# A two-block transformer kernel: convolution taps on VectorE unpinned and given low priority, eight tap tiles for GpSimd, 30 diagonal taps on TensorE, and broadcasts without diagonals

## The chip, the core and the metric

The kernel runs on one core of one Trainium2 chip. The core has five engines that work side by side, each through its own queue in order: TensorE (PE in the profile, with PEld for its weight loads), VectorE (DVE), ScalarE (ACT), GpSimd (POOL) and SyncE (SP, which issues most DMAs). Results of TensorE go to PSUM, eight banks of 128 x 512 fp32; all other tiles lie in SBUF. The metric is the device time of one execution in microseconds, the median of several runs.

## What is computed

Two blocks over a sequence of 512 tokens of width 1024, all in fp32. The first block: RMS norm, a mixer of four mLSTM heads and four gated-linear-attention heads (both directions), a projection, then a feed-forward part with a three-tap convolution. The second block has two layers: a pool-and-convolution mixer, cross-attention to a memory of 256 rows and a feed-forward part; then latent attention, cross-attention and a feed-forward part again; last a norm. Two places matter here.

In the mLSTM each head and direction has, per query t and key s, a decay that is an exponential of a stabilised difference:

```python
d_intra = where(causal, b[t] - b[s] + i[s], -inf)
m_t = maximum(m_inter, max(d_intra, -1))
s = einsum('bhtd,bhsd->bhts', q_, k_) * exp(d_intra - m_t)
```

In the pool-and-convolution mixer the convolution has 31 taps per channel over 512 channels, which the kernel holds as four chunks of 128 channels (one per partition):

```python
gl = glu_a * sigmoid(glu_b)
cv = causal_dwconv(gl, dw_w) + dw_b        # 31 taps per channel
yb = silu(layernorm(cv, ln_g, ln_b))
return concatenate([ya, yb], -1) @ w_out   # ya: pooled windows of 2, 4, 8, 16
```

## The kernel before

Activations are kept transposed, features on partitions and 512 tokens along the free axis. Every large product is made from two-part numbers: `split` (L200 to L216) writes a high part with ScalarE (L208, `wh`) and the remainder with VectorE (L209, `wl`), and `mm3` (L237 to L239) runs three float32r products high x high, low x high, high x low. So each weight tile of 128 x 1024 that TensorE uses costs one operation on ScalarE and one on VectorE before it.

The program is traced in Python and a list scheduler of the language lays out each engine's queue ahead of time: an operation carries a priority from its place in the program, `tc.high_priority(offset=n)` moves that priority by n places earlier (a negative n later), and `tc.keep_in_program_order` (called `pin` here) ties an operation behind the one traced just before it on its engine. The queues are then fixed; on the chip an engine whose next operation waits stands still.

`bcast_cols` (L312 to L326) makes a row that is the same on all partitions from a column: four times, VectorE multiplies the identity by the column (L317, `dg`), and TensorE multiplies a matrix of ones by that diagonal (L318); ScalarE copies the result out as `rb` (L325). It is called at 13 places, in the norms at the ends of the stages.

In the mLSTM, `mx` (L750) holds the running maxima that two scans write (L760, L762). Two additions follow (L764, L765), whose result TensorE transposes (L768). For each of eight head-and-direction pairs `ml_build` spreads one row of `mx` over all partitions with an fp32 product, `mb` (L907), which ScalarE then takes through the exponential (L921).

In the pool-and-convolution stage (`pool_mix`, from L1232) the order of the work is written out in `ORDER`: blocks of the input projection (`a`, `b`, `p`), the pooled windows' products (`w`), and pieces of the next cross-attention's memory projection as filling (`k`). Between them, `all_taps` hands out the taps of chunks 0 to 3, eight at a time. A tap goes one of three ways: `own` taps (`POOLC`, 9, 8, 5 and 3 of the chunks) are scaled by ScalarE into a tile `cm` (L1294, four tiles) and added by GpSimd (L1295), both pinned; `dia` taps (`PEC`, 0, 8, 8 and 8) are fp32 products of TensorE with a diagonal matrix (L1272, L1279); all others are VectorE's, which multiplies and adds into the same PSUM bank (L1303), pinned. L1307 joins the sums into `cv`. `means` (L1368) sums each `cv` over channels with TensorE; after the fourth, the layer norm follows: mean (L1411), difference (L1415), squares (L1417), their sums (L1419), `rsqrt_mean`, `bcast_cols`, gain (L1436) and SiLU (L1438), beside the first products of the output projection.

Of the kernel before, what the change touches and what calls it, by code (L numbers as in the profile page):

```python
# [10 lines left out]
F32 = mybir.dt.float32  # L11
F32R = mybir.dt.float32r
U8 = mybir.dt.uint8
I32 = mybir.dt.int32
ACTF = mybir.ActivationFunctionType
ALU = mybir.AluOpType
# [3 lines left out]
P = 128  # L20
S = 512
# [2 lines left out]
DEC = (3, 6)  # L24
LAG = 0
POOLC = (9, 8, 5, 3)
PEC = (0, 8, 8, 8)
ORDER = 'a1 p3 b2 k a2 p2 k b3 a3 p1 k p0 w3 k w2 w1 w0'
KVS = (0, 2, 0, 1)
TURN = (((2,), (0,)), ((1, 3),))  # L30
# [32 lines left out]
def kernel(ctx: ExitStack, tc: tile.TileContext, A, out, stages=ALL_STAGES):  # L63
    nc = tc.nc
    V, SC, GP, PE, DMA = nc.vector, nc.scalar, nc.gpsimd, nc.tensor, nc.sync
# [25 lines left out]
    def ptmp(shape=(P, S), dtype=F32, tag="t", bufs=6):  # L91
        return tp.tile(list(shape), dtype, tag=tag, bufs=bufs, name=tag)
# [11 lines left out]
    ident = const.tile([P, P], F32, name="ident")  # L104
    ones = const.tile([P, P], F32, name="ones")
# [206 lines left out]
    def bcast_cols(r, m=4, pool=None, stay=False):  # L312

        ps = pm("aux", (P, m * P))
        for j in range(m):
            dg = ptmp((P, P), tag="dg", bufs=2)
            V.tensor_scalar(out=dg, in0=ident, scalar1=r[:, j:j + 1], scalar2=None, op0=ALU.mult)  # L317
            PE.matmul(ps[:, j * P:(j + 1) * P], lhsT=ones, rhs=dg, start=True, stop=True)  # L318
        if stay:
            return ps  # L320
        if pool is None:
            rb = ptmp((P, m * P), tag="rb", bufs=2)
        else:
            rb = pool.tile([P, m * P], F32, tag="rbp", name="rbp")
        SC.activation(out=rb, in_=ps, func=ACTF.Copy)  # L325
        return rb  # L326
# [332 lines left out]
    def mix_heads(mp, layers):  # L659
# [19 lines left out]
        with nc.allow_non_contiguous_dma(reason="a column of 128 for each of 8 feature tiles"):  # L679
            (SC, DMA, GP)[LQ].dma_start(out=par[:, base["mix_pre"]:base["mix_pre"] + KD],  # L680
                         in_=A["norm_mix_pre"].rearrange("o (z p) -> p (o z)", p=P))
# [7 lines left out]
                      in_=wi[:, g0:g0 + 16].rearrange("(k p) c -> p k c", p=P))  # L689
        DMA.dma_start(out=wst[:, :, 16:48],  # L690
                      in_=wi[:, l0:l0 + 32].rearrange("(k p) c -> p k c", p=P))
# [36 lines left out]
        ps = opened[1][0]  # L728
# [6 lines left out]
        def log_sigmoid(dst, x, t):  # L735
# [11 lines left out]

        bt = ptmp()
        um = ptmp()
        mx = mp.tile([P, S], F32, name="mx")  # L750
        GP.memset(um, 0.0)
        GP.memset(mx, 0.0)
        bo = one.to_broadcast([P, S])
# [1 line left out]
                             op0=ALU.mult, op1=ALU.add)  # L755
# [5 lines left out]
                             op0=ALU.mult, op1=ALU.max)  # L761
        V.tensor_tensor_scan(out=mx[64:68, ::-1], data0=bo[32:36], data1=um[32:36, ::-1],  # L762
                             initial=0.0, op0=ALU.mult, op1=ALU.max)
        V.tensor_tensor(out=um[64:68], in0=bt[0:4], in1=mx[0:4], op=ALU.add)  # L764
        V.tensor_tensor(out=um[96:100], in0=bt[64:68], in1=mx[64:68], op=ALU.add)  # L765
        ps = pm("aux")
# [4 lines left out]
        for d in range(2):  # L771
            V.tensor_copy(umc[:, :, 4 * d:4 * d + 4], psv[:, :, 32 * d:32 * d + 4])
            SC.activation(out=em[:, :, 4 * d:4 * d + 4], in_=psv[:, :, 64 + 32 * d:68 + 32 * d],
                          func=ACTF.Exp, scale=-1.0)
# [125 lines left out]
        def span(d, j):  # L900
            return (j * P, S) if d == 0 else (0, (j + 1) * P)

        def ml_build(h, d):
            q, k2 = qs[h], khl[h]
            mb = pm("aux")
            r0 = 64 * d + h
            PE.matmul(mb, lhsT=ident[:, r0:r0 + 1].to_broadcast([P, P]), rhs=mx, start=True,  # L907
                      stop=True)
            e = w5("e", (P, 1280))
            for js in GRP[d]:  # L910
                st = pm("st")
                o0 = OFF[d][js[0]]
                tot = 0
                for j in js:
                    a, b = span(d, j)
                    o = OFF[d][j] - o0
                    ks = slice(j * P, (j + 1) * P)
                    for i in range(2):
                        PE.matmul(st[:, o:o + b - a], lhsT=k2[:, i, ks], rhs=q[:, a:b],
                                  start=i == 0, stop=i == 1)  # L920
                    SC.activation(out=e[:, OFF[d][j]:OFF[d][j] + b - a], in_=mb[:, a:b],  # L921
                                  func=ACTF.Exp, scale=-1.0,
                                  bias=umc[:, j, 4 * d + h:4 * d + h + 1])
                    tot += b - a
                sl = slice(o0, o0 + tot)
                V.tensor_tensor(out=e[:, sl], in0=st[:, :tot], in1=e[:, sl], op=ALU.mult)
                for j in js:
                    a, b = span(d, j)
                    o = OFF[d][j] + (0 if d == 0 else b - a - P)
                    sg = 1 if d == 0 else -1  # L930
                    GP.affine_select(out=e[:, o:o + P], in_=e[:, o:o + P], pattern=[[sg, P]],
                                     compare_op=ALU.is_ge, fill=0.0, base=0,
                                     channel_multiplier=-sg)
            return e
# [300 lines left out]
    def pool_mix(nm, nxt, pp, fill):  # L1235
# [32 lines left out]
        def diagonals(c):  # L1268
            dgs[c] = []
            for j in dia[c]:  # L1270
                dg = pp.tile([P, P], F32, tag="dgc", bufs=10, name="dgc")
                SC.activation(out=dg, in_=ident, func=ACTF.Copy, scale=pc("dw_w", 4 * j + c))  # L1272
                dgs[c].append(dg)

# [6 lines left out]

        pin = tc.keep_in_program_order

        def conv(c):
            gl, ps = gls[c], cps[c]
            c2 = pp.tile([P, S], F32, tag="c2", bufs=2, name="c2")
            SC.activation(out=c2, in_=gl[:, 0:S], func=ACTF.Identity, scale=pc("dw_w", c),
                          bias=pc("dw_b", c))
            fresh = not PEC[c]
            for j in range(1, 31):  # L1290
                w = pc("dw_w", 4 * j + c)
                if j in own[c]:
                    t = pp.tile([P, S], F32, tag="cm", bufs=4, name="cm")
                    pin(SC.activation(out=t, in_=gl[:, j:j + S], func=ACTF.Copy, scale=w))  # L1294
                    pin(GP.tensor_tensor(out=c2, in0=c2, in1=t, op=ALU.add))  # L1295
                elif j in dia[c]:
                    continue
                elif fresh:
                    V.tensor_scalar(out=ps, in0=gl[:, j:j + S], scalar1=w, scalar2=None,
                                    op0=ALU.mult)  # L1300
                    fresh = False
                else:
                    pin(V.scalar_tensor_tensor(out=ps, in0=gl[:, j:j + S], scalar=w, in1=ps,  # L1303
                                               op0=ALU.mult, op1=ALU.add))
                yield
            cv = pp.tile([P, S], F32, name=f"cv{c}")
            V.tensor_tensor(out=cv, in0=ps, in1=c2, op=ALU.add)  # L1307
            cvs[c] = cv
            yield
# [104 lines left out]
        for c in range(4):  # L1414
            V.tensor_tensor(out=cvs[c], in0=cvs[c], in1=mean, op=ALU.subtract)  # L1415
            sq = ptmp(tag="sq", bufs=3)
            SC.activation(out=sq, in_=cvs[c], func=ACTF.Square)  # L1417
            for j in range(4):
                PE.matmul(pss[:, j:j + 1], lhsT=sq[:, j * P:(j + 1) * P], rhs=ones[:, 0:1],  # L1419
                          start=c == 0 and j == 0, stop=c == 3 and j == 3)  # L1420
# [10 lines left out]
        r = rsqrt_mean(pss, S, 4)  # L1431
# [3 lines left out]
        for c in range(4):  # L1435
            V.scalar_tensor_tensor(out=cvs[c], in0=cvs[c], scalar=pc("ln_g", c), in1=lb,  # L1436
                                   op0=ALU.mult, op1=ALU.mult)
# [383 lines left out]
    pcs, pp = ExitStack(), []  # L1821
# [78 lines left out]
```

## Time and profile before

| | us |
|---|---|
| median of 3 runs | 2183.96 |
| lowest and highest | 2183.51 and 2189.16 |
| the profiled execution | 2181.3 |
| its span in the trace | 2178.9 |

| engine | busy us | share of the span |
|---|---|---|
| TensorE | 2105.1 | 97% |
| TensorE's weight loads | 1768.7 | 81% |
| VectorE | 1208.9 | 55% |
| ScalarE | 945.9 | 43% |
| GpSimd | 372.7 | 17% |

The profiled execution is 2.7 us below the median, and its span leaves out 2.4 us around the work. Shares are averages over stages that differ; a stage is read in windows of time. The mLSTM lies at about 40 to 200 us, the pool-and-convolution stage at about 786 to 935 us. The granted clock is that of TensorE as a share of its full speed.

### The profile page before, as it was taken

What the parts mean: (1) busy time and instruction counts of PE and PEld (TensorE: products, weight loads), DVE (VectorE), ACT (ScalarE), POOL (GpSimd) and SP (SyncE); (2) the same over time, 40 slices, a digit from 0 to 9 for tenths busy, and PEclk for the clock granted to TensorE, in tenths of its full rate; (3) what the DMA queues carried; (4) which work ended last, traced back from release to release, by engine and by line L of the source; (5) the groups of instructions that cost most, each with busy time, mean ns of one, the idle gap of its engine ahead of it and who ended that gap; (6) DMA issues with size and microseconds to landing.
All of it is one profiled execution on the core that took longest, in us unless ns stands there. A gap on an engine that the chain in (4) does not pass through costs nothing.

```text
span 2178.9 us, 27908 instructions
## 1 busy us (share of the span) xinstructions
PE 2105.1 (97%) x10807; PEld 1768.7 (81%) x10807; DVE 1208.9 (55%) x1795; ACT 945.9 (43%) x1561; POOL 372.7 (17%) x414
## 2 busy tenths in 40 slices
PE   7999899999999999899999999999999999999998
PEld 6888778788888876778888888888888888888887
DVE  6655755655532378755665554337885565555432
ACT  5765554433332454343443333226774343333322
POOL 2113411211100047020111110112322011111010
PEclk9999999999999999999999999999999999999999
DMA  5543245233333332532233333331124223333331
GB/s 144 161 152 114 88 145 165 73 102 97 97 112 98 114 102 82 174 118 77 73 92 97 97 97 96 116 107 45 35 93 151 78 58 87 97 97 97 94 102 66
DMA packets 369984, 222.88 MB, mean 102 GB/s; under 512 B 22407, under 2 KB 351036, under 8 KB 369852
## 3 DMA queue, kind: packets, MB, share of 16 engines
q1 hardware_dynamic: 366304, 219.65, 33.9%
q8 instruction: 85, 1.39, 0.3%
q10 hardware_dynamic: 3228, 1.42, 0.2%
q14 instruction: 47, 0.39, 0.1%
q0 software_dynamic: 320, 0.04, 0.0%
HBM read 201.41 MB, written 19.66 MB: 101 GB/s over the span
## 4 chain that ended last, share of the span: by engine, by line
PE 80%; DVE 8%; ACT 5%; issue 3%; POOL 1%; DMA 1%; SPq 0%; ACTq 0%; POOLq 0%; DVEq 0%
PE mm L239 21%; PE mm L237 21%; PE mm L238 21%; PE st L237 2%; PE st L238 2%; PE st L239 2%; PE nd L237 2%; PE nd L238 2%; PE nd L239 1%; DVE wl L209 1%; ACT wh L208 1%; DVE cv L1303 1%; ACT pr L1727 1%; PE aux L318 1%; DVE c L1726 1%
## 5 line engine op out<-in xcount | busy, mean ns | idle before, releaser
L208 ACT ACTIVATE wh<-ws 128x1024 fp32r<-128x1024 f32 (+2 forms) x352 | 361.3, 1029 | 774.1 <-PE mm L239 556.7
L209 DVE TENSOR_TENSOR wl<-ws,wh 128x1024 fp32r<-128x1024 f32 (+2 forms) x352 | 421.9, 1200 | 335.7 <-ACT wh L208 335.4
L237 PE MATMUL mm<-a,wh 128*128 128x512 f32 (+1 forms) x1364 | 530.2, 389 | 2.8 <-ACT a L208 1.3
L239 PE MATMUL mm<-a,wh 128*128 128x512 f32 (+1 forms) x1364 | 528.1, 387 | 1.6 <-DVE a L215 1.6
L238 PE MATMUL mm<-a,wl 128*128 128x512 f32 (+1 forms) x1364 | 527.9, 387 | 0.8 <-DVE wl L209 0.8
L237 PEld LDWEIGHTS mm<-a,wh 128*128 128x128 f32 x1364 | 258.4, 190 | 54.7 <-ACT a L208 1.7
L239 PEld LDWEIGHTS mm<-a,wh 128*128 128x128 f32 x1364 | 258.2, 189 | 54.0 <-DVE a L215 3.4
L238 PEld LDWEIGHTS mm<-a,wl 128*128 128x128 f32 x1364 | 258.3, 189 | 51.6 <-DVE wl L209 2.0
L237 PE MATMUL mm<-hh,wh 128*128 128x512 f32 (+1 forms) x550 | 209.6, 381 | 0.0
L238 PE MATMUL mm<-hh,wl 128*128 128x512 f32 (+1 forms) x550 | 209.3, 381 | 0.0
L239 PE MATMUL mm<-hl,wh 128*128 128x512 f32 (+1 forms) x550 | 209.3, 381 | 0.0
L283 POOL TENSOR_TENSOR sq<-sq 128x512 f32<-128x512 f32 x60 | 92.4, 1540 | 646.6 <-ACT sq L278 562.0
L1203 POOL TENSOR_TENSOR t<-t,rb 128x512 f32<-128x512 f32 x66 | 85.1, 1290 | 613.9 <-ACT t L1202 613.9
L1190 DVE TENSOR_TENSOR t<-mm,rb 128x512 f32<-128x512 f32 x64 | 44.2, 691 | 147.2 <-PE mm L239 147.2
L1206 DVE TENSOR_TENSOR t<-mm,t 128x512 f32<-128x512 f32 x65 | 45.0, 692 | 140.4 <-POOL t L1203 140.4
L239 PEld LDWEIGHTS mm<-hl,wh 128*128 128x128 f32 x550 | 103.4, 188 | 19.8
L238 PEld LDWEIGHTS mm<-hh,wl 128*128 128x128 f32 x550 | 103.4, 188 | 19.7
L237 PEld LDWEIGHTS mm<-hh,wh 128*128 128x128 f32 x550 | 103.4, 188 | 19.6
L237 PE MATMUL mm<-wh,a 128*128 128x256 f32 x346 | 100.1, 290 | 2.3 <-DVE Kl L209 2.3
L239 PE MATMUL mm<-wl,a 128*128 128x256 f32 x346 | 99.6, 288 | 1.8 <-DVE wl L209 1.7
L1199 DVE SCALAR_TENSOR_TENSOR t<-t,par 128x511 f32<-128x511 f32 (+1 forms) x132 | 98.7, 748 | 3.2 <-ACT t L1195 0.9
L1202 ACT ACTIVATE t<-t 128x512 f32<-128x512 f32 x66 | 41.7, 632 | 133.6 <-DVE t L1199 133.5
(469 smaller groups left out, 3553.3 us busy)
## 6 DMA issues: line engine op xcount, KB each, us to landing
ws<-in_ffn_w_up_dram SPq DMA_DIRECT2D x110, 512.0 KB, 3.8
ws<-in_ffn_w_down_dram SPq DMA_DIRECT2D x48, 512.0 KB, 3.8
ws<-in_xa_wkv_dram SPq DMA_DIRECT2D x32, 512.0 KB, 4.4
ws<-in_w_in_dram SPq DMA_DIRECT2D x24, 512.0 KB, 5.0
ws<-in_ffn_w_gate_dram SPq DMA_DIRECT2D x22, 512.0 KB
ws<-in_ffn_w_down_dram SPq DMA_DIRECT2D x24, 384.0 KB, 3.4
ws<-in_xa_wq_dram SPq DMA_DIRECT2D x16, 512.0 KB, 5.5
ws<-in_xa_wo_dram SPq DMA_DIRECT2D x16, 512.0 KB, 3.7
```

The source lines that it names most:

```text
L208: SC.activation(out=hi, in_=src, func=ACTF.Copy)
L209: eng.tensor_tensor(out=lo, in0=src, in1=hi.bitcast(F32), op=ALU.subtract)
L237: PE.matmul(ps, lhsT=lh, rhs=rh, start=start, stop=False)
L238: PE.matmul(ps, lhsT=ll, rhs=rh, start=False, stop=False)
L239: PE.matmul(ps, lhsT=lh, rhs=rl, start=False, stop=stop)
L283: GP.tensor_tensor(out=self.acc, in0=self.acc, in1=self.new, op=ALU.add)
L318: PE.matmul(ps[:, j * P:(j + 1) * P], lhsT=ones, rhs=dg, start=True, stop=True)
L1190: V.tensor_tensor(out=g, in0=pg, in1=rb, op=ALU.mult)
L1199: V.scalar_tensor_tensor(out=cv[:, o], in0=g[:, i], scalar=w, in1=cv[:, o], op0=ALU.mult, op1=ALU.add)
L1202: SC.activation(out=ge, in_=cv, func=func)
L1203: GP.tensor_tensor(out=ge, in0=ge, in1=rb, op=ALU.mult)
L1206: V.tensor_tensor(out=h, in0=pu, in1=ge, op=ALU.mult)
```

## The change

Four edits. (1) `bcast_cols` has no diagonal any more: the column itself, read as if it were 128 equal columns, is the stationary operand and the identity the moving one. (2) `mx` moves to a temporary tile and is split into a float32r tile `mhl`, high parts in its own rows (one ScalarE copy) and remainders 32 rows below (two VectorE subtractions); a selector `sel`, the identity plus itself moved by 32, adds both parts in one float32r product per `mb`, where there was an fp32 product. (3) GpSimd's taps get eight tiles in a fixed round, five of `cm` and three borrowed from the ring of `sq`; VectorE's taps are no longer pinned, and their priority is 120 places later than their place in the program. (4) `PEC` goes from 24 to 30 diagonal taps, so VectorE's taps go from 71 to 65 (one of them, L1299, opens chunk 0), and the ring of diagonals from 10 to 11 tiles.

```diff
-PEC = (0, 8, 8, 8)
+PEC = (0, 9, 10, 11)
@@ bcast_cols
         for j in range(m):
-            dg = ptmp((P, P), tag="dg", bufs=2)
-            V.tensor_scalar(out=dg, in0=ident, scalar1=r[:, j:j + 1], scalar2=None, op0=ALU.mult)
-            PE.matmul(ps[:, j * P:(j + 1) * P], lhsT=ones, rhs=dg, start=True, stop=True)
+            PE.matmul(ps[:, j * P:(j + 1) * P], lhsT=r[:, j:j + 1].to_broadcast([P, P]), rhs=ident,
+                      start=True, stop=True)
@@ mix_heads
-        mx = mp.tile([P, S], F32, name="mx")
+        mx = ptmp()
+        mhl = mp.tile([P, S], F32R, name="mx")
+        sel = ptmp((P, P), F32R, tag="dg", bufs=2)
...
+        SC.activation(out=mhl, in_=mx, func=ACTF.Copy)
+        for r0 in (0, 64):
+            V.tensor_tensor(out=mhl[r0 + 32:r0 + 36], in0=mx[r0:r0 + 4],
+                            in1=mhl[r0:r0 + 4].bitcast(F32), op=ALU.subtract)
+        V.tensor_tensor(out=sel[:, 0:96], in0=ident[:, 0:96], in1=ident[:, 32:P], op=ALU.add)
@@ ml_build
-            PE.matmul(mb, lhsT=ident[:, r0:r0 + 1].to_broadcast([P, P]), rhs=mx, start=True,
+            PE.matmul(mb, lhsT=sel[:, r0:r0 + 1].to_broadcast([P, P]), rhs=mhl, start=True,
                       stop=True)
@@ diagonals
-                dg = pp.tile([P, P], F32, tag="dgc", bufs=10, name="dgc")
+                dg = pp.tile([P, P], F32, tag="dgc", bufs=11, name="dgc")
@@ pool_mix
+        def tap_tiles():
+            while True:
+                for n in range(8):
+                    yield ptmp(tag="sq", bufs=3) if n % 3 == 2 or n == 7 else \
+                        pp.tile([P, S], F32, tag="cm", bufs=5, name="cm")
+
+        cms = tap_tiles()
@@ conv
-                    t = pp.tile([P, S], F32, tag="cm", bufs=4, name="cm")
+                    t = next(cms)
                     pin(SC.activation(out=t, in_=gl[:, j:j + S], func=ACTF.Copy, scale=w))
                     pin(GP.tensor_tensor(out=c2, in0=c2, in1=t, op=ALU.add))
...
-                    pin(V.scalar_tensor_tensor(out=ps, in0=gl[:, j:j + S], scalar=w, in1=ps,
-                                               op0=ALU.mult, op1=ALU.add))
+                    with tc.high_priority(offset=-120):
+                        V.scalar_tensor_tensor(out=ps, in0=gl[:, j:j + S], scalar=w, in1=ps,
+                                               op0=ALU.mult, op1=ALU.add)
```

## Rows read from the trace of the kernel before

**Rows 1.** The page, busy time: engine, us, share of the span, instructions.
```profile
PE 2105.1 (97%) x10807; PEld 1768.7 (81%) x10807; DVE 1208.9 (55%) x1795; ACT 945.9 (43%) x1561; POOL 372.7 (17%) x414
```
**Rows 2.** The page, the chain that ended last: shares of the span by engine.
```profile
PE 80%; DVE 8%; ACT 5%; issue 3%; POOL 1%; DMA 1%; SPq 0%; ACTq 0%; POOLq 0%; DVEq 0%
```
**Rows 3.** Waits of PE, whole span: total us, times, longest us.
```profile
PE aux L1368 <- DVE cv L1307: 7.0, 3, 3.2
...
PE aux L768 <- DVE t L765: 3.5, 1, 3.5
PE aux L318 <- DVE dg L317: 3.5, 6, 1.0
...
PE mm L239 <- DVE wl L209: 1.7, 3, 0.7
```
**Rows 4.** Windows: length, then busy us of PE, PEld, DVE, ACT, POOL, clock, DMA.
```profile
50.00:200.00 150.00, 143.55 (x1032) 129.56 (x1031) 92.72 (x199) 105.79 (x216) 27.53 (x51) 0.99 0.45 139
802.60:907.00 104.40, 95.96 (x472) 72.81 (x470) 87.53 (x114) 44.84 (x69) 52.62 (x49) 0.98 0.31 99
835.40:838.80 3.40, 3.36 (x4) 1.51 (x5) 3.33 (x5) 1.03 (x2) 2.09 (x3) 0.50 0.47 154
913.60:920.60 7.00, 7.00 (x28) 6.13 (x27) 1.94 (x5) 1.64 (x3) 0.00 (x0) 0.52 0.97 315
```
**Rows 5.** Timeline of PE, pool-and-convolution stage: start, us, operation, idle before it.
```profile
835.44 2.04 PE L1368 MATMUL aux<-cv,ones 128*128 128x512 f32 x2 [3.03 <-DVE cv L1307]
907.02 2.03 PE L1368 MATMUL aux<-cv,ones 128*128 128x512 f32 x2 [3.25 <-DVE cv L1307]
913.12 1.16 PE L1419 MATMUL aux<-ones,sq 128*128 128x1 f32 x8 [2.79 <-ACT sq L1417]
930.86 0.50 PE L237 MATMUL mm<-a,wh 128*128 128x512 f32 x1 [1.32 <-ACT a L208]
```
**Rows 6.** Chain that ended last, by time: start, us on the chain, what.
```profile
31.49 0.64 ACT t L737
42.59 0.69 DVE t L765
120.86 0.86 PE aux L907 x2
779.84 0.23 PE op L237
802.78 6.87 PE cv L1279 x16
```
**Rows 7.** Lines L907, L317, L318: instructions, ns minimum, median, maximum.
```profile
L907 PEld LDWEIGHTS aux<-mx,ident x16: 187/188/337, 66.6 to 161.3; 128*128 128x128 f32 x16
L317 DVE TENSOR_SCALAR dg<-ident,c x52: 278/286/316, 18.7 to 1808.7; 128x128 f32<-128x128 f32 x52
L318 PEld LDWEIGHTS aux<-dg,ones x104: 186/189/192, 22.6 to 1809.1; 128*128 128x128 f32 x104
L318 PE MATMUL aux<-dg,ones x104: 270/275/377, 22.8 to 1809.2; 128*128 128x128 f32 x104
```
**Rows 8.** Line L1303, VectorE's taps: instructions, ns minimum, median, maximum.
```profile
L1303 DVE SCALAR_TENSOR_TENSOR cv<-gl,par,cv x70: 740/756/757, 800.8 to 904.5; 128x512 f32<-128x512 f32 x70
```
**Rows 9.** Timeline of DVE, pool-and-convolution stage: start, us, operation, idle before.
```profile
815.17 0.69 DVE L1251 TENSOR_TENSOR t<-mm,rb 128x512 f32<-128x512 f32 x1 [4.51 <-PE mm L239]
...
828.57 1.22 DVE L209 TENSOR_TENSOR wl<-ws,wh 128x1024 fp32r<-128x1024 f32 x1
...
875.37 0.69 DVE L209 TENSOR_TENSOR wl<-ws,wh 128x512 fp32r<-128x512 f32 x1 [2.05 <-ACT wh L208]
```
**Rows 10.** Timeline of POOL, same stage: start, us, operation, how many.
```profile
818.78 14.83 POOL L1295 TENSOR_TENSOR c<-c,cm 128x512 f32<-128x512 f32 x9
...
885.02 1.30 POOL L1295 TENSOR_TENSOR c<-c,cm 128x512 f32<-128x512 f32 x1
```
**Rows 11.** Waits of all engines, 780 to 935 us: total us, times, longest.
```profile
ACT cm L1294 <- POOL c L1295: 4.8, 5, 1.6
```

## The prediction, as it stood before the result was known

> **What bounds the kernel now.** I read the page's busy times first, then the chain that ended last, then TensorE's waits, then windows of the two stages that the change touches, and last the timelines of single engines there. TensorE is busy for 97% of the span and VectorE for 55% [rows 1], and 80% of the chain is TensorE's own work [rows 2]. So two things alone move the end: time that TensorE's queue works, and time that it stands still. All its recorded idle time is 2178.9 - 2105.1 = 73.8 us, spread over the whole program; a change that touches two stages can reach only a part of it. Its largest wait is L1368, the channel sums of a finished convolution chunk, for `cv`: 7.0 us in three waits; L768 behind the running maxima has 3.5 us, L318 behind the diagonals 3.5 us [rows 3]. From 802.6 to 907 us, the convolution, TensorE is idle for 104.4 - 95.96 = 8.4 us, so L1368 is nearly all of that; VectorE is busy for 87.5 us of the 104.4 [rows 4], which is the densest it is anywhere for so long. An idle time costs more than itself: after 3.03 us the pair of L1368 at 835.44 took 2.04 us [rows 5] where an fp32 pair of the same shape takes 0.86 [rows 6], and the granted clock of the 3.4 us from 835.4 was 0.50 (1.2 GHz for 2.4), which loses 1.7 us more [rows 4]; the 3.25 us before 907.02 have the same pair at 2.03 us behind them [rows 5].
>
> **Edit 2, the maxima.** An `mb` is two passes of 0.43 us, 0.86 in all; a float32r product of the same 512 columns holds TensorE for 0.23 us [rows 6]. Its weights are a repeated column before and after, and loading such costs 188 ns, like any others (189) [rows 7]. Eight times 0.63 is 5.04 us less work for TensorE. In the window from 50 to 200 us, where they lie, TensorE is busy for 143.55 of 150 us [rows 4], so I count 96% of it: **-4.8 us** (bounds -5.0, and -2.5 if half of it falls into waits). Against that stand one ScalarE copy, two VectorE subtractions and the selector. The nearest rows are a ScalarE operation of 128x512 at 0.64 and a four-row VectorE addition at 0.69 (L765), on the chain at 42.59 us [rows 6]; the selector is like a `dg`, 0.29 [rows 7]. L764 can run while ScalarE copies, but the two subtractions come before L765 in the program, and TensorE already waits 3.5 us for L765 [rows 3]. So 2 x 0.69 lie on the path, and a little of the selector: **+1.5 us** (bounds 0, if L765 goes first, and 0.64 + 1.38 + 0.29 = 2.3). Who waits there is L768 and all that TensorE has queued behind it. The first `mb` comes over 20 us later, at 66.6 us [rows 7], so that its own new wait, for `mhl`, costs nothing. `mx` in a temporary tile takes one of six; at that time others have had their last reader, so I put nothing on it, and at worst one later step waits for one scan.
>
> **Edit 1, the broadcasts.** 52 operations of 286 ns leave VectorE, 14.9 us in all; TensorE's 104 passes stay with the same shape and load [rows 7]. VectorE's time is off the path except where TensorE waits for a diagonal, 3.5 us in six waits [rows 3]. After the change TensorE waits for the column itself, one VectorE operation earlier; what is queued behind it is the same. I take 70% of the waits: **-2.5 us** (bounds 0 and -3.5).
>
> **Edits 3 and 4, the convolution.** Six more diagonals are six more fp32 products: 16 passes took 6.87 us [rows 6], so 0.86 each, **+5.15 us** of work that TensorE cannot avoid. They take six taps of 756 ns [rows 8], 4.5 us, from VectorE. The six more ScalarE diagonals lie in an engine that is busy for 45 of 104 us [rows 4] and cost nothing.
>
> What the freed taps can give back is read from VectorE's idle time. It stands still four times for long between 810 and 876 us, for 4.51, 2.85, 3.70 and 2.05 us, the first and the last in [rows 9], 13.1 us together, each time for a gate, a split or a part of a window that TensorE or ScalarE had not delivered, while taps whose data lay ready were pinned behind it. Unpinned they fill these gaps. With the six taps gone VectorE is 13.1 + 4.5 = 17.6 us ahead at the last `cv`. GpSimd must keep up: its last addition ends at 886.3 us [rows 10], 20 us before the last `cv` is awaited, and the tiles that made ScalarE wait 4.8 us for GpSimd [rows 11] are doubled. So the waits of L1368 should go. I keep 1.5 of the 7.0 us, since TensorE's queue is laid out ahead of time and each earlier chunk may still come a little late: **-5.5 us**; the two stretches at half clock go with them, 2 x 1.7: **-3.4 us**. Of TensorE's waits for `wl`, 1.7 us in all [rows 3], I take **-0.7**. Net: 5.15 - 5.5 - 3.4 - 0.7 = **-4.45 us**. The layer norm behind the last `cv` keeps its cost in this sum: 2.79 us before the squares' sums, 1.32 before the last products [rows 5], and 7 us at clock 0.52 [rows 4], of which half is lost, together 7.6 us. It shrinks only if the last `cv` comes so early that TensorE still has other products to run. The bounds of this part: nothing comes back, +5.15; everything does, with the tail, 5.15 - 7.0 - 3.4 - 1.3 - 7.6 = -14.2.
>
> One row bears on VectorE and GpSimd side by side. A `wl` at 828.57 us took 1.22 us [rows 9] in the middle of nine GpSimd additions without a gap [rows 10], which is no more than others take. The Trainium skill (SBUF — State Buffer, section "SBUF: two separate sides") says that a VectorE operation with two SBUF inputs and a GpSimd operation that reads SBUF take a shared pair of ports in turn, and the later one waits for the whole of the other. By that rule, more additions in a row would speak against this change; this row does not agree.
>
> **The sum.** -4.8 + 1.5 - 2.5 - 4.45 = -10.25 us. Against the profiled execution, 2181.3 us, that is 2171.0. The median of the runs lies 2.7 us higher, and I carry the difference over: 2183.96 - 10.25 = **2173.7 us**. About 0.3%, 6.55 us, is what a measurement of this kernel can tell from no change: faster is under 2177.4, slower over 2190.5. All bounds on one side give 2183.96 - 5.0 - 3.5 - 14.2 = 2161.3, on the other 2183.96 - 2.5 + 2.3 + 5.15 = 2188.9.
>
> **The rivals.** *The waits stay (0.23).* The queues are fixed by a plan; if VectorE runs later than planned by as much as now, L1368 waits as now. For it: all three of its waits are of this kind, and `po` (L1330) and GpSimd's additions stay pinned behind taps. Against it: 17.6 us of lead. Then the diagonals cost 5.15 and perhaps 1 us comes back: -4.8 + 1.5 - 2.5 + 4.15 = -1.65, **2182.3 us**. *The tail goes too (0.14).* If the 17.6 us of lead reach the layer norm, its 7.6 us are hidden as well: **2166.1 us**. *Taps ahead of weights, slower (0.07).* A plan that takes a `wl` to be ready later than it is puts a tap before it, and TensorE waits. 19 weight splits start between 798.9 and 907 us; each one caught costs up to one tap, 0.756 us, once its reserve is used up. With the waits of the first rival, from (6.55 + 1.65) / 0.756 = 11 of them the kernel is slower by over 0.3%; at 14 it is **2192.9 us**. Against it: low priority puts the taps behind, and TensorE's waits for `wl` are 1.7 us today [rows 3]. *Turns at the ports (0.04).* If each of the 19 splits waited for half of a GpSimd addition of 1.30 us [rows 10], VectorE would lose 12.4 of the 17.6 us; with half of L1368's waits and one half-clock stretch back, 5.2 us more than forecast, **2178.9 us**. This is the rule of the Trainium skill's page on SBUF named above. The row of 828.57 us speaks against it, and TensorE's share of the work doesn't change by it.
>
> **How the numbers follow.** The forecast, some 2168 to 2179 us, has 0.52. Faster: 0.50 of it and the hidden tail, 0.64. Within 0.3%: the rest of it, the waits that stay, the ports and a part of the fourth, 0.31. Slower: 0.05. The range, 2164 to 2184 us, takes in the first rival and most of the second, and leaves out the fourth.
>
> **What would show it.** Right: L907 as one pass of about 0.23 us, eight of them; L317 gone and L318's wait with it; L1303 64 times, in the place of the four idle stretches; L1368 without a wait over 1.5 us and no half clock at its side; 12 more passes of L1279. Wrong: L1368 still waiting 5 us or more (the plan's error, not VectorE's load, set it); new waits for `wl` in the convolution; L768 waiting 2 us longer than 3.5, or not at all longer.

## The result, and the profile after

The changed kernel took **2163.36 us** in the median of five runs (2163.23 to 2167.51), the kernel before 2187.45 us in five runs beside it (2183.51 to 2189.16). The ratio is **0.9897** with an interval of 0.9883 to 0.9911: 22.5 us less (the two medians differ by 24.1; differences below go by the ratios unless medians are named), where the prediction had 10.25 us less. A second measurement later, with more runs of the kernel before beside it (17), gave 0.9930 [0.9912, 0.9947], 15.3 us less (run e9 below). Both lie clear of no change.

The profiled execution of after took 2167.51 us (span 2165.7), that of before 2181.3 (span 2178.9). The pair of profiles therefore shows 13.2 us of span. The profile of before is quicker than each of its five timed runs, that of after is the slowest of its five; a part of the difference between the medians stands in neither profile, and runs e1 and e2 below show a stretch that can hold some of it.

Busy times of after (the page; as [rows 1]), and TensorE's waits over the whole span (as [rows 3]: total us, times, longest):

```profile
PE 2099.2 (97%) x10811; PEld 1770.3 (82%) x10811; DVE 1196.4 (55%) x1740; ACT 947.9 (44%) x1568; POOL 375.1 (17%) x414
```
```profile
PE st L1098 <- DVE xb L1087: 5.5, 2, 3.9
...
PE aux L775 <- DVE t L772: 3.3, 1, 3.3
PE aux L316 <- DVE c L309: 2.5, 4, 0.9
PE aux L1385 <- DVE cv L1324: 2.4, 2, 1.7
...
PE mm L239 <- DVE wl L209: 1.0, 1, 1.0
```

TensorE's idle time falls from 73.8 to 2165.7 - 2099.2 = 66.5 us. The channel sums of the convolution chunks (L1368, now L1385) wait 2.4 us in two waits, not 7.0 in three. The wait of 2.8 us ahead of the squares' sums (L1419, now L1436) is in the list no more. The first line is no cost of the change, though it was 3.0 us before: L1098 lies in the gated-linear-attention part, and kernels whose program is that of before up to there waited 3.0 (e4), 5.5 (e12) and 6.4 us (e3) for the same `xb`. It scatters from one execution to the next.

Along the program the lead of after grows so: the last `mb` ends 6.7 us earlier (162.3 to 155.7 us), the pool-and-convolution stage opens 5.2 us earlier (793.0 to 787.8), and it ends, at the copy of the second broadcast behind it, 13.8 us earlier (976.3 to 962.5). So that stage gives 8.5 us. The 5.2 us are less certain than they look: four kernels with the program of before up to this point (before, e3, e4, e12) open the stage at 791.4 to 797.2 us, the eight with edits 1 and 2 at 787.8 to 792.9. The stage itself is used below as the yardstick: from the first `rb` copy of it to the one behind it, 183.3 us before, 174.7 after. Windows (length; busy us of PE, PEld, DVE, ACT, POOL; clock; DMA), first of before, then of after:

```profile
793.00:976.30 183.30, 170.15 (x801) 132.43 (x800) 131.10 (x182) 83.54 (x127) 70.14 (x61) 0.96 0.39 122
```
```profile
50.00:200.00 150.00, 144.20 (x1072) 134.16 (x1072) 91.87 (x197) 106.52 (x218) 27.29 (x51) 0.99 0.48 146
787.80:962.50 174.70, 169.71 (x809) 132.68 (x808) 127.51 (x168) 85.03 (x133) 70.45 (x61) 0.98 0.42 128
797.30:892.00 94.70, 91.31 (x423) 67.04 (x422) 81.67 (x105) 43.41 (x72) 52.51 (x50) 1.00 0.28 88
904.30:911.10 6.80, 6.80 (x22) 5.65 (x21) 0.90 (x5) 0.00 (x0) 1.02 (x1) 0.50 0.59 188
```

In the stage TensorE's idle time falls from 183.3 - 170.15 = 13.2 to 174.7 - 169.71 = 5.0 us, and the time at half clock from 13.7 us (three stretches) to 6.8 (the one at 904.3). That is 8.2 + 3.4 us of gain against 5.15 us for six more diagonals, 6.5 us net; the other 2.0 of the 8.5 us are not assigned to a row. The convolution itself ran at full clock (1.00 from 797.3 to 892; 0.98 in [rows 4]).

The timeline of TensorE in after (start, us, operation, idle before it; as [rows 5]):

```profile
826.02 1.10 PE L1385 MATMUL aux<-cv,ones 128*128 128x512 f32 x2 [1.72 <-DVE cv L1324]
...
842.87 1.12 PE L1385 MATMUL aux<-cv,ones 128*128 128x512 f32 x2 [0.65 <-DVE cv L1324]
...
865.99 1.02 PE L1385 MATMUL aux<-cv,ones 128*128 128x512 f32 x2
...
892.82 1.02 PE L1385 MATMUL aux<-cv,ones 128*128 128x512 f32 x2
900.63 1.84 PE L1436 MATMUL aux<-ones,sq 128*128 128x1 f32 x16
...
917.82 0.50 PE L237 MATMUL mm<-a,wh 128*128 128x512 f32 x1 [1.10 <-ACT a L208]
```

No pair of L1385 takes 2.03 us any more, the time of such a pair at half clock [rows 5]. The third and the fourth `cv` are there when TensorE comes to them. Most of all: L1436 at 900.63 has no idle time before it. It follows directly on filling products for the next memory projection, the last of them at 900.51. In before those products had run out when the last `cv` came, and TensorE stood still for 2.79 us [rows 5].

VectorE's idle time did not go away, it moved. Its two long waits in the convolution of after (the timeline of DVE; as [rows 9]):

```profile
835.74 3.92 DVE L1320 SCALAR_TENSOR_TENSOR cv<-gl,par,cv 128x512 f32<-128x512 f32 x5 [3.77 <-PE cv L1286]
...
866.19 3.92 DVE L1320 SCALAR_TENSOR_TENSOR cv<-gl,par,cv 128x512 f32<-128x512 f32 x5 [6.38 <-PE cv L1286]
```

Four waits of 13.1 us for gates and splits became two of 10.2 us for the diagonals' products (L1279, now L1286): the taps of a chunk add into the bank that those products open. Set against the start of the stage, the last `cv` comes at 892.6 - 787.8 = 104.8 us where it came at 907.0 - 793.0 = 114.0 before: **9.2 us of lead**, not the 17.6 that the prediction counted.

### The profile page after: what moved, and what is told of

Read it like the earlier page. It is cut to its first block, busy times and chain, and to the rows that moved or that the text cites. A ratio compares the mean times of both kernels' runs of the same rounds, so it can differ in the third digit from the quotient of the medians.

```text
span 2165.7 us, 27870 instructions
## 1 busy us (share of the span) xinstructions
PE 2099.2 (97%) x10811; PEld 1770.3 (82%) x10811; DVE 1196.4 (55%) x1740; ACT 947.9 (44%) x1568; POOL 375.1 (17%) x414
## 4 chain that ended last, share of the span: by engine, by line
PE 81%; DVE 8%; ACT 5%; issue 4%; POOL 1%; DMA 0%; SPq 0%; POOLq 0%; ACTq 0%; DVEq 0%
PE mm L239 21%; PE mm L237 21%; PE mm L238 21%; PE st L237 2%; PE st L239 2%; PE st L238 2%; DVE wl L209 2%; PE nd L237 2%; PE nd L238 1%; PE nd L239 1%; DVE cv L1320 1%; PE cv L1286 1%; ACT wh L208 1%; ACT pr L1744 1%; DVE c L1743 1%
```

## The experiments

Two theories were set against each other. By the first, the parts add up and each is as large as its term of the sum. By the second, the convolution part is worth far more than its term, since an earlier last `cv` also takes the waits and the half clock of the layer norm's tail. Four kernels do one part of the change alone on the kernel before; their runs share the runs of the kernel before (2184.56 us).

**The broadcasts alone** (edit 1).

```diff
-            dg = ptmp((P, P), tag="dg", bufs=2)
-            V.tensor_scalar(out=dg, in0=ident, scalar1=r[:, j:j + 1], scalar2=None, op0=ALU.mult)
-            PE.matmul(ps[:, j * P:(j + 1) * P], lhsT=ones, rhs=dg, start=True, stop=True)
+            PE.matmul(ps[:, j * P:(j + 1) * P], lhsT=r[:, j:j + 1].to_broadcast([P, P]), rhs=ident,
+                      start=True, stop=True)
```

> The kernel before with the first edit alone: column broadcasts without diagonals. Theory A, the terms of the prediction: 2.5 us faster than the kernel before (0 to 3.5), since TensorE's waits for the diagonals (3.5 us) go. Theory B, the gain of 24 us in the medians comes from work taken off VectorE at the ends of stages, which the terms missed: 8 us or more faster. In the trace: rb of each norm 0.5 to 1 us earlier than its reciprocal root was before.

Measured: 2181.84 us, ratio 0.9985 [0.9975, 0.9995], so -3.3 us (-1.1 to -5.5); forecast -2.5. The broadcasts wait 2.4 us in four waits, where they waited 3.5 in six: 1.1 of the 3.3 us can be seen there. The copies `rb` start earlier, as expected: at most of the 11 places 1.25 to 1.4 us behind the end of the reciprocal root, where it was 2.0 to 2.1. Against this stands a wait that grew: in every run with edit 1 TensorE waits 3.6 to 4.6 us for `x` (L480, in the first block), in every run without 0.8 to 1.7 us; two waits for an `a` behind it shrink from 2.5 to 0.7 us in all. The profile of e1 shows something else. The waits around the last `cv` are those of before to the hundredth, and behind them the clock stays at half for 20.5 us in one piece (timeline, then window):

```profile
907.54 1.12 PE L1367 MATMUL aux<-cv,ones 128*128 128x512 f32 x2 [3.25 <-DVE cv L1306]
913.22 1.01 PE L1418 MATMUL aux<-ones,sq 128*128 128x1 f32 x4 [2.79 <-ACT sq L1416]
```
```profile
908.80:929.30 20.50, 17.71 (x57) 14.82 (x58) 6.93 (x15) 5.63 (x11) 1.02 (x1) 0.50 0.59 201
```

20.5 us at 0.50 cost 10 us; the two stretches at the same place in the profiled execution of before, 3.4 and 6.8 us, cost 5. The order of TensorE's products in this stage is that of before up to the broadcast behind the layer norm (in e2, which has the same stretch, all through the stage). So the tail, which the prediction took at 7.6 us from one profile, can cost up to 5 us more in another execution, an estimate from these stretches; the whole stage took 186.4 us in e1 and 187.1 in e2, for 183.3.

**The maxima alone** (edit 2, its core).

```diff
+        SC.activation(out=mhl, in_=mx, func=ACTF.Copy)
+        for r0 in (0, 64):
+            V.tensor_tensor(out=mhl[r0 + 32:r0 + 36], in0=mx[r0:r0 + 4],
+                            in1=mhl[r0:r0 + 4].bitcast(F32), op=ALU.subtract)
...
-            PE.matmul(mb, lhsT=ident[:, r0:r0 + 1].to_broadcast([P, P]), rhs=mx, start=True,
+            PE.matmul(mb, lhsT=sel[:, r0:r0 + 1].to_broadcast([P, P]), rhs=mhl, start=True,
```

> The kernel before with the second edit alone: running maxima split in two parts, one float32r product for each spread row. Theory A, the terms: 4.8 us less work for TensorE, 1.5 us more in front of the transposes, 3.3 us faster. Theory B, that shorter products let ScalarE and VectorE start earlier in each head as well: 6 us or more faster by the end of the mLSTM. In the trace: eight products of 0.23 us in place of 0.86, the wait of the transposes 5 us in place of 3.5.

Measured: 2180.88 us, ratio 0.9978 [0.9966, 0.9990], -4.8 us (-2.2 to -7.4); forecast -3.3. Timelines of DVE and PE:

```profile
40.94 0.68 DVE L772 TENSOR_TENSOR t<-t 4x512 f32<-4x512 f32 x1
41.65 0.68 DVE L773 TENSOR_TENSOR t<-t 4x512 f32<-4x512 f32 x1
42.37 1.38 DVE L769 TENSOR_TENSOR mx<-t,mx 4x512 fp32r<-4x512 f32 x2
```
```profile
42.48 0.63 PE L776 MATMUL aux<-ident,t 128*128 128x128 f32 x4 [3.37 <-DVE t L773]
```

The plan put both additions ahead of the two subtractions that are traced before them (L769 after L772 and L773), and the transposes wait 3.37 us, as before (3.54). So the trace shows the +1.5 us of the prediction to be zero; without it, the term is -4.8. The interval alone would not tell -4.8 from -3.3. This execution has 20.5 us at half clock in the tail as well, from 904.5.

**The convolution alone** (edits 3 and 4), and then **without the six diagonals** (edit 3 alone, `PEC` left at 24).

```diff
-PEC = (0, 8, 8, 8)
+PEC = (0, 9, 10, 11)        # e3 only
...
-                    t = pp.tile([P, S], F32, tag="cm", bufs=4, name="cm")
+                    t = next(cms)
...
-                    pin(V.scalar_tensor_tensor(out=ps, in0=gl[:, j:j + S], scalar=w, in1=ps,
-                                               op0=ALU.mult, op1=ALU.add))
+                    with tc.high_priority(offset=-120):
+                        V.scalar_tensor_tensor(out=ps, in0=gl[:, j:j + S], scalar=w, in1=ps,
+                                               op0=ALU.mult, op1=ALU.add)
```

> The kernel before with the third and fourth edit alone: free low-priority taps, eight tap tiles, 30 diagonal taps. Theory A, the terms: 4.5 us faster, the waits of the channel sums mostly gone, the layer norm's tail as it was. Rival, the tail goes too: 12 us or more faster. Rival, the waits stay: 4 us slower.

> As the run with the third and fourth edit, but with 24 diagonal taps as before, so that VectorE keeps 71 taps and TensorE has 5.15 us less work. Theory A: the freed taps alone give back 9.6 us, and the six diagonals cost 5.15 of them, so this run is about 5 us faster than the run with 30 diagonals. Rival, VectorE is what bounds the convolution once its taps are free: this run is no faster than the one with 30 diagonals, or slower, and the channel sums wait again.

Measured: e3 2168.91 us, 0.9935 [0.9917, 0.9953], **-14.2 us** (forecast -4.45, its lowest bound -14.2); e4 2166.28 us, 0.9914 [0.9900, 0.9927], **-18.8 us**. The three parts, -3.3, -4.8 and -14.2, make -22.3 us, the whole as first measured -22.5; as measured again in e9 it is -15.3, so whether the parts add up is not settled. The convolution is where the forecast fell short: its part alone moved by 9.75 us more than its term. The difference of e3 and e4 is the price of six diagonals: 4.6 us by the ratios and 2.6 by the medians, where the prediction had 5.15. The intervals of the two runs overlap, but their stages agree (172.6 and 168.7 us, below).

The sums and the whole region of the convolution and its tail in e4:

```profile
828.61 1.10 PE L1378 MATMUL aux<-cv,ones 128*128 128x512 f32 x2 [1.33 <-DVE cv L1317]
843.78 1.13 PE L1378 MATMUL aux<-cv,ones 128*128 128x512 f32 x2 [0.69 <-DVE cv L1317]
```
```profile
828.00:932.00 104.00, 99.40 (x511) 78.21 (x512) 82.44 (x115) 47.89 (x72) 34.44 (x34) 1.00 0.43 139
```

The clock is 1.00 through all 104 us, tail included, and no wait stands before the squares' sums. The stage takes 168.7 us in e4 and 172.6 in e3 (183.3 before), with 5.5 and 5.0 us of idle TensorE and no half clock. Against the profile of before, e3 thus has 2.79 us of wait and 6.8 us at half clock less in the tail; with half of the latter lost time, that is 6.2 us that the prediction had left in place. The 3.5 us that remain of the 9.75 can come from longer stretches in other executions of before, as in e1 and e2; no run shows that they do.

**Parts taken out of the change.** Four kernels start from the changed kernel: the diagonals back at 24; the taps of VectorE pinned again; GpSimd's taps back in four `cm` tiles; the taps free but at the priority of their place. They were run together, beside 2183.62 us.

```diff
-PEC = (0, 9, 10, 11)
+PEC = (0, 8, 8, 8)                                                  # e5
...
-                    with tc.high_priority(offset=-120):
-                        V.scalar_tensor_tensor(out=ps, ...)
+                    pin(V.scalar_tensor_tensor(out=ps, ...))         # e6
+                    V.scalar_tensor_tensor(out=ps, ...)              # e8
...
-                    t = next(cms)
+                    t = pp.tile([P, S], F32, tag="cm", bufs=4, name="cm")   # e7
```

> The changed kernel with 24 diagonal taps as before (ring of ten). Theory A, the six diagonals are plain work of TensorE even in the changed kernel, since VectorE has time to spare once its taps are free: 4.5 us faster than the changed kernel, about 22 us + 4.5 = 27 us faster than the kernel before. Rival, six more taps make VectorE late at the last join: the wait of the channel sums comes back by 3 us or more and the run is no faster than the changed kernel.

> The changed kernel with VectorE's taps pinned again, but the eight tiles and the 30 diagonals kept. Theory A, the freed place of the taps is what removes the waits of the channel sums and the half-clock stretches: the waits are back (over 5 us), a half-clock stretch lies behind the last channel sum, and the run is 12 us or more slower than the changed kernel. Rival, the tiles do it, by no longer holding ScalarE: within 4 us of the changed kernel.

> The changed kernel with four tap tiles as before, taps free at low priority, 30 diagonals. Theory A: the tiles matter little, within 3 us of the changed kernel; ScalarE waits for GpSimd 4 to 5 us again without anybody waiting for it. Rival, ScalarE's wait delays weights and windows that the freed taps now depend on: 5 us or more slower, with new waits of TensorE for weights.

> The changed kernel with VectorE's taps free but at their own place's priority, not 120 places later. Theory A, that it is the lifted pin and not the lower priority: within 3 us of the changed kernel. Rival, that taps at their own priority run ahead of the weights' remainders: TensorE's waits for these grow to 5 us or more, and the run is 5 us or more slower than the changed kernel.

Since three of the four came out alike, the changed kernel itself was measured once more (e9), beside 2185.01 us, together with two kernels with still fewer diagonals (`PEC = (0, 6, 6, 6)` and `(0, 4, 4, 4)`, the rest of the change kept).

> The changed kernel once more, beside the kernel before and the three runs of this call, so that 30, 18 and 12 diagonals are compared on one chip. All theories: about 2163 to 2166 us, 0.99 of the kernel before; in the trace no half-clock stretch of more than 7 us in the convolution's tail.

> The changed kernel with 18 diagonal taps (6 each of chunks 1 to 3). Theory A, diagonals are plain TensorE work while VectorE has time to spare: 12 x 0.86 = 10 us less work than the changed kernel, of which at least 5 us show. Rival, VectorE's last join then comes after TensorE has run out of filling: the wait of the last channel sum returns (3 us or more), and with it a half-clock stretch, so that the run is no faster than with 24 diagonals, or slower.

> The changed kernel with 12 diagonal taps (4 each). VectorE has 18 taps, 13.6 us, more than in the changed kernel. Theory A holds on only if VectorE's idle time covers them: 15 us less work of TensorE. Rival, past the point where VectorE is full: the channel sums wait 6 us or more, and the run is slower than with 18.

| kernel | median us | ratio [interval] | stage us | TensorE idle | at half clock |
|---|---|---|---|---|---|
| e9, the change again | 2168.70 | 0.9930 [0.9912, 0.9947] | 172.9 | 5.7 | 3.4 |
| e6, taps pinned | 2168.36 | 0.9931 [0.9914, 0.9947] | 176.0 | 7.1 | 6.8 |
| e7, four tiles | 2168.50 | 0.9931 [0.9910, 0.9952] | 174.4 | 7.0 | 3.4 |
| e8, own priority | 2166.92 | 0.9925 [0.9908, 0.9942] | 173.8 | 6.3 | 3.4 |
| e5, 24 diagonals | 2160.41 | 0.9891 [0.9874, 0.9908] | 168.9 | 5.6 | 3.4 |
| e10, 18 diagonals | 2162.33 | 0.9901 [0.9885, 0.9918] | 168.1 | 9.7 | 3.4 |
| e11, 12 diagonals | 2174.99 | 0.9954 [0.9940, 0.9969] | 179.1 | 15.4 | 30.7 |

The changed kernel came out slower than expected (2163 to 2166 us), and nearer to its three variants. Three things follow.

First, **no single part of edit 3 carries it**. With the pin back, the gain should have gone by at least 12 us if lifting the pin alone had made it; against e9 nothing went that the intervals can tell, and the stage is 3.1 us longer (1.3 longer than in the first profile of the change, 174.7). The theory fell. The pinned kernel also does without the long waits of L1368: with 30 diagonals and eight tiles the sums wait 1.4 us, but VectorE's old order brings a new wait elsewhere, ahead of a pooled window's product at 899.8 us, until a split of VectorE ended (waits of PE in the stage of e6):

```profile
PE mm L237 <- DVE t L209: 3.4, 1, 3.4
PE aux L1384 <- DVE cv L1323: 1.4, 1, 1.4
```

That the three parts stand in for each other, so that with any one of them gone the others still relieve VectorE, is a reading of these runs; no run takes two of them out. Four tiles instead of eight, or the taps' own priority instead of the low one, differ from the change by 1.5 and 0.9 us of stage, less than its own two profiles differ (174.7 and 172.9), and by nothing in the times. The tiles are not without effect, though: with four of them ScalarE waits 4.7 us for GpSimd again, and the sums wait 4.4 us, for 3.1 in e9.

Second, **the six diagonals are a loss here**: e5 has the lowest median of all, 23.2 us under before (forecast 27), and its stage takes 168.9 us, 4.0 less than e9's.

Third, where fewer diagonals stop paying. From 30 to 18 diagonals TensorE has 12 products less, 10.3 us, and 6.4 us of them arrive in the median (e9 and e10); the rest comes back as new waits behind splits. At 12 diagonals the waits win (waits of PE in the stage, first e10, then e11):

```profile
PE mm L237 <- ACT a L208: 2.7, 1, 2.7
PE mm L237 <- DVE a L215: 2.5, 1, 2.5
PE aux L1385 <- DVE cv L1324: 2.1, 2, 1.1
```
```profile
PE mm L237 <- DVE a L215: 5.4, 2, 3.1
PE mm L237 <- ACT ph L208: 2.8, 1, 2.8
PE aux L1436 <- ACT sq L1434: 2.1, 1, 2.1
PE aux L1385 <- DVE cv L1324: 2.0, 2, 1.5
```

Note what waits: not the sums, which stay at 2 us, but products behind splits of ScalarE and VectorE. Those behind `ph` waited for VectorE: the pooled window that `ph` is split from comes at 891.25 us in e11, behind five taps that end at 889.08, a weight split and one more tap. The wait behind `a` that ends at 876.0 was not made by the taps (timeline of DVE in e11):

```profile
868.90 3.38 DVE L1320 SCALAR_TENSOR_TENSOR cv<-gl,par,cv 128x512 f32<-128x512 f32 x5
872.33 1.23 DVE L209 TENSOR_TENSOR wl<-ws,wh 128x1024 fp32r<-128x1024 f32 x1
873.72 1.23 DVE L209 TENSOR_TENSOR wl<-ws,wh 128x1024 fp32r<-128x1024 f32 x1 [0.17 <-ACT wh L208]
...
875.20 1.40 DVE L215 SCALAR_TENSOR_TENSOR a<-mm,par,a 128x512 fp32r<-128x512 f32 x2
```

The taps end at 872.3 us, before the products that `a` reads are done (873.0 and 873.7). Between them and `a` stand two weight splits, and ScalarE ends its own halves of these at 872.30 and 873.69 and its halves of `a` at 874.5 and 875.1. The product that waits opens a new `mm` bank, of which this stage has three: by the code it waits until a bank has been read, not for `a` as an operand. In e11 the last `cv` comes 109.2 us behind the start of the stage, and the wait ahead of the squares' sums is back (2.1 us, L1436); it was 2.79 at 114.0 us in before, and there is none at 107.9 us in e6 or sooner in the others.

Beside the waits of e11 stand 30.7 us at half clock. The turning point lies between 18 and 12 diagonals.

**Does the wait make the half clock?** The last run keeps the kernel before, and lets TensorE work through the wait ahead of the last `cv` with products that nobody reads; what filling is left is traced ahead of them (`drain(fill)`), so the order behind the last sum changes a little too.

```diff
+                if c == 3:
+                    pin(m)
...
+        drain(fill)
+        dm = pm("cv")
+
+        def keep_busy(n):
+            for _ in range(n):
+                pin(PE.matmul(dm, lhsT=ident, rhs=cvs[2], start=True, stop=True))
+
+        keep_busy(2)
...
+        keep_busy(3)
```

> The kernel before with five fp32 products of an identity ahead of the last channel sum, whose result nobody reads: TensorE works (4.3 us) where it waited (3.25 us). Theory A, what the wait costs is mostly the half clock behind it, which the tail then keeps for 7 to 20 us: the clock stays at 1.00 behind the last sum, the run is 3 to 9 us faster than the kernel before in spite of the added work. Rival, the clock falls anyway, or its cost is small: 1 us slower or no difference.

Measured: 2185.81 us, ratio 1.0002 [0.9991, 1.0013]: nothing. The waits before the last sum and before the squares' sums are gone from the timeline, and so is the first stretch at half clock, the one beside that sum: from 844.3 the clock is 1.00 until 919.4. Then it falls all the same (windows, and the timeline of PE):

```profile
912.00:919.40 7.40, 5.54 (x28) 3.53 (x27) 6.03 (x10) 5.03 (x9) 0.00 (x0) 1.00 0.60 181
919.40:929.60 10.20, 10.20 (x33) 8.65 (x33) 1.13 (x6) 0.00 (x0) 1.02 (x1) 0.50 0.67 232
```
```profile
916.47 0.50 PE L237 MATMUL mm<-a,wh 128*128 128x512 f32 x1 [1.72 <-ACT a L214]
917.28 0.95 PE L1430 MATMUL aux<-ones,sq 128*128 128x1 f32 x8
...
936.25 0.62 PE L237 MATMUL mm<-a,wh 128*128 128x512 f32 x1 [1.77 <-ACT a L208]
```

That is 7.2 us behind the last `cv` (912.2), the place of the second stretch in before (913.9 - 907.0 = 6.9), and it runs 10.2 us where that ran 6.8. A third stretch of 3.4 us follows at 936.5, behind the wait of 1.77. So behind the last `cv` the clock is at half for 13.6 us, where it was 10.2 in before. The theory that the 3.25 us before the last sum bring the half clock of the tail falls; with them gone, the first 3.4 us of it are gone in this execution, and no more. What stands before the second fall is a stretch in which TensorE is busy for 5.54 of 7.40 us, with a wait of 1.72 us in it. Nothing was saved: five products without use are 4.3 us of TensorE, and idle time in the stage is 3.8 us less (9.4 for 13.2); the stage takes 186.0 us.

## Why the prediction was right in direction, and where its sum was off

The sign, the places and the mechanism held: faster, by TensorE's work in the mLSTM, by the waits for diagonals and by the sums' waits. The size did not: the time lies 0.6 us under the low end of the range (2164) in the first measurement and inside it in the second (2168.7; forecast 2173.7), and the change is 22.5 or 15.3 us where 10.25 was forecast.

- **The maxima, -4.8 us: right.** L914 is one pass, eight times (its record of 0.39 us overlaps the next: the one at 78.91 us has its successor at 79.14, 0.23 us later); alone it gave -4.8. TensorE's busy share in the mLSTM's window is 144.20 of 150 us, 143.55 before [rows 4], so the freed time was filled.

```profile
L914 PE MATMUL aux<-mx,dg x8: 388/396/628, 66.2 to 155.2; 128*128 128x512 f32 x8
```

- **Their chain, +1.5 us: wrong, it is zero.** The step assumed the traced order; the plan moved the additions ahead. The prediction named this end of the bound (0, if L765 goes first) and chose the other.
- **The broadcasts, -2.5 us: -3.3 alone, within the interval.** By the waits the step was too bold: 1.0 us of 3.5 went in after, not 70%. The column itself comes late too, from the same chain. Most copies `rb` come 0.7 us sooner behind their column; how much of this reaches the end is not known.
- **Six diagonals, +5.15 us: right in size** (4.6 by the ratios of e3 and e4, 6.9 by the medians of e5 and e9 set against their own runs of before; twelve gave 6.4 by e9 and e10, since waits came back).
- **The sums' waits, -5.5: -4.6, right in size**, 0.9 us more kept than said and one wait of 1.72 us over the limit set. **`wl`, -0.7: right** (1.0 us in one wait). The half clock beside the sums is gone in this profile; in e5, e7, e8 and e9 one stretch of 3.4 us stays at the first sum, at 826 to 830 us.
- **The lead of 17.6 us: wrong in its working.** It took all of VectorE's idle time as ready to be filled. The freed taps filled the old gaps, and 10.2 us of new ones opened, because free taps of a chunk still cannot start before the diagonals' products of their chunk. Also VectorE's own operations became longer, see below. The lead is 9.2 us.
- **"The layer norm behind the last `cv` keeps its cost": this is the step that failed**, and it mis-sized the largest term. The convolution was given -4.45 us; alone it brought -14.2. The condition stood in the prediction, that it shrinks only if TensorE still has other products to run, and 9.2 us of lead were enough for it. In after the wait of 2.79 us is gone; in e3 and e4, and in e5, e7, e8 and e9, the tail's half clock is gone as well (after itself has 6.8 us of it). That the tail goes too was a rival with 0.14; its mechanism is what the runs show, though with 9.2 us of lead and not 17.6.
- **The tail's price was read from one execution.** 7.6 us in the profile of before, up to 5 more in others (e1, e2), where the same queue kept the half clock for 20.5 us. Single runs of before lie between 2179.1 and 2190.8 us, of after between 2163.2 and 2173.9.

The rivals: *the waits stay* and *taps ahead of weights* are out for 30 diagonals; the second shows at 12, though for `ph`, not for `wl`. *Turns at the ports* decided nothing, but the row that was read against it was only half of the story: the split at 828.57 us went first, and the GpSimd addition beside it ran from 828.63 to 830.91, 2.28 us where a lone one takes 1.30. In the same place of after, a `wl` takes 1.22 us beside a GpSimd addition that takes 2.18, and 12 us earlier two splits take 2.27 and 1.78 us beside additions of 1.29 and 2.17 (timelines of DVE, then of POOL):

```profile
815.11 2.27 DVE L209 TENSOR_TENSOR wl<-ws,wh 128x1024 fp32r<-128x1024 f32 x1
817.30 1.78 DVE L209 TENSOR_TENSOR pl<-po,ph 128x512 fp32r<-128x512 f32 x1
...
827.71 1.22 DVE L209 TENSOR_TENSOR wl<-ws,wh 128x1024 fp32r<-128x1024 f32 x1
```
```profile
815.00 1.29 POOL L1311 TENSOR_TENSOR c<-c,sq 128x512 f32<-128x512 f32 x1
816.37 2.17 POOL L1311 TENSOR_TENSOR c<-c,cm 128x512 f32<-128x512 f32 x1
...
827.88 2.18 POOL L1311 TENSOR_TENSOR c<-c,sq 128x512 f32<-128x512 f32 x1
```

The one that starts later becomes longer. The split at 815.11 ends at 817.38, 1.09 us behind the end of the addition that ran when it started (816.29). The next addition ends 1.16 us behind that split (818.54), the next split 0.55 us behind that addition (819.09), and the addition at 827.88 ends 1.12 us behind the `wl` beside it. Each is a little less than the operation takes alone (1.22, 1.30, 0.69 and 1.30), as if it had waited for the rest of the other. The additions at 818.78 in [rows 10] also took 14.83 / 9 = 1.65 us each, where a lone one takes 1.30. Summed over the convolution, VectorE's splits of `wl` and `pl` are 5.4 us over their shortest time in after, 2.3 us in before, at most 1.1 us in one. This agrees with the rule of the Trainium skill that the prediction weighed (SBUF — State Buffer, section "SBUF: two separate sides"). So the prediction read its row wrongly when it found that the rule did not hold here; its price of 12.4 us for 19 splits was too high, since only 7 of the 19 in after were held up.

**What stays open.** Edit 3's parts were not run singly on the kernel before (tiles alone, pin alone), nor 30 diagonals with everything else as before; so how the 18.8 us of e4 divide between the lifted pin and the tiles is not known, only that each can be missed while the rest is there. Nor is it shown that the tail alone makes up the 9.75 us by which the convolution beat its term; 6.2 us of them are seen. What sets the length of a half-clock stretch in the tail is not settled. Nor is why the change gave 22.5 us in the first measurement and 15.3 in the second, whose intervals just miss each other (0.9911 and 0.9912).

## What to carry to other kernels

When the last input of a stage comes earlier, ask first what TensorE is still doing at that time: if filling products are left, the waits and the half clock behind that input go too, and a term that "keeps its cost" may be the largest of the sum. A feeder's idle time is no lead as long as the work that would fill it waits for another engine itself; count only what is ready. And where work is moved to the engine that sets the end, try one step less: here 24 diagonals with free taps had lower medians than 30 both times, by 2.6 us without edits 1 and 2 and by more with them, and 12 were too few.

## What the runs showed of the hardware

The same queue of TensorE, with the same waits of 3.25 and 2.79 us, ran 3.4 and 6.8 us at a granted clock of 0.50 in one execution and 20.5 us in two others (e1, e2). Two edits that leave the order of TensorE's products there as it was thus have a profile whose tail has twice as much half clock, so such a term read from one profile needs a bound for the longer stretch. And filling the longest wait with work took away the first stretch alone (e12): the second began at about the same distance behind the last `cv` (7.2 us, 6.9 before) and ran 10.2 us. VectorE's splits and GpSimd's additions held each other up: whichever began later ended 1.1 us (`wl`, an addition) or 0.55 us (`pl`) behind the other's end.
